# All eight channel groups of branch A as seven products, one filler job per head, one gate tile, two weight and three kq buffers

## The chip, the cores and the metric

The kernel runs on one core of a Trainium2 chip. The metric is the device time of one execution in microseconds (us), from profiler counters on the chip; for the kernel before it is the median of three runs. Engines: PE is TensorE (matmuls; PEld its weight loads), DVE VectorE, ACT ScalarE, POOL GpSimd, SP SyncE, which issues most DMAs.

## The reference, cut to what matters

One layer, for a prompt of 1024 rows and for 8 sample rows (1032 in all), in fp32. Only this much bears on the change:

```
h    = rmsnorm(x, norm_pre) * (1 + scale) + shift
proj = h @ w_in                      # 1024 -> 10256 columns
hA, cA, bA, zA, qkv, zB, beta, alpha, gA, gB = split(proj)
a_conv = causal conv of width 3 over (cA * hA)
yA = ((bA * a_conv) * silu(zA)) @ w_out_a
q, k, v = split(silu(causal conv of width 4 over qkv))      # 8 heads of 128
o, S = gated delta rule over each head (a chain over the rows)
yB = (rmsnorm(o) * silu(zB)) @ w_out_b
merged = sigmoid(gA) * yA + sigmoid(gB) * yB
y  = x + gate * rmsnorm(merged @ w_o, norm_post)
```

hA, cA, bA and zA have 1024 columns each: eight groups of 128 channels. The last rows of the convolutions and the states S are outputs too.

## The kernel before, in words

**Precision.** Each fp32 operand of a large matmul is split into a high and a low part (fp32r), so a product is three matmuls: high by high, low by high, high by low. x is held as xh and xl, a weight as whi and wlo.

**Jobs.** A job (`run`, line 692) projects x on 128 columns of w_in: three groups of 344 rows, eight k blocks, three terms, 72 matmuls of 128x128 by 344 columns into the PSUM tile `pm_t`, of which there are four. While job i runs, the weights of job i+2 are loaded (`w_load`, 671, tile `wraw`, three buffers) and those of i+1 are split (`w_split`: whi by ACT, wlo by DVE, two buffers each). After each group of 24 matmuls a function of the job evacuates it. The list of jobs is built at lines 1358 to 1372, 60 in all: for each head h six jobs, namely k, q, v, two of the 16 column blocks of the merge gates (`gate_job`, 1132: three copies by ACT to a tile and a store) and z (`zb_job`, 1118: three silus by ACT into the gate tile `sz`, two buffers); then three channel groups of branch A (`branch_a_jobs`, 1146; SG = 3) with four jobs each (h, c, b, z).

**Head chains.** Behind the jobs of a head run generators. `qkv_job` (800) copies a projection to `raw`, and does the convolution and the silu into `kq` (k and q, two buffers) or vT; the k of head h waits until head h-2 is done. `decay_gen` (837) makes the decay factors DA and DB with exponentials on ACT. `delta_gen` (864) transposes k and q, squares them (`junk`, `ssk`), makes the 128x128 matrices of the eight chunks, inverts them by blocks (tiles Tw, Tn, Un, T11, U, Qs; not before head h-1 is done), and then goes through the chunks in a chain. For each chunk:

```
pk, po = kq.T @ S          # PE "pa_t<-S,kq", two matmuls
X  = pk * nx + vp          # DVE
pv = U.T @ X               # PE "pa_t<-X,U"
vn = copy(pv)              # ACT
pS, po += kd, DA by vn     # PE "pa_t<-vn,kd" and "pa_t<-vn,DA"
S  = S * egl + pS          # DVE
on, so = copy(po), sum of squares    # ACT
```

After the eighth chunk the flag "done" is set; then come the norm (`rsqrt`, a row of small DVE steps on so and ro), the scaling of `on` (1024 columns, DVE), eight transposes on PE (`pa_t<-ident,on`) and two passes on DVE that multiply by the head's gate `sz`; then the flag "out". `zb_job` makes head h's gate only when "out" of head h-2 is set, as there are two tiles. `sample_gen` (1208) and `sample_norm_gen` (1275) do the same for the sample rows with z_s, a copy of z's last columns.

**Order.** A planner (`Sched`, `Strand`) keeps a clock per engine by its own cost table. After each k block `slot()` runs a step of every generator that is due by the planner's PE clock; `force(cond)` advances them until a condition holds. The generators' PE steps so fall between the projection matmuls, and the tile framework then orders each engine's instructions. PE, ACT, DVE and SP each work through theirs in order; all instructions carry the line of one helper, L121.

**Products.** The other five channel groups (t = 3 to 7) are not jobs. `products` (1575) computes, for each, the four 128-column blocks by Strassen's scheme in Winograd's form: x (two halves of rows by two of k) times four weight blocks in seven half-size products P1, P2, P6, P7, P4, P5, P3. Each product has 48 matmuls of 258 columns, a group 336. `weight_gen` (1404) loads and combines the weights (also from the `wraw` tag: `wsum`), `block_gen` (1493) builds the sums of x blocks T1 to T4 (tiles thi, tlo), DVE adds the products (`evacuate`), and `finish_group` does the convolution and gating. `to_products` is hooked three jobs before the end of the list and first drains the head generators. Then `products_b` (1633) does yB @ w_out_b the same way (14 units; weights and yB blocks come by DMA), then eight jobs follow for w_out_a, and last w_o with the post norm by blocks of rows.

Of the kernel before, what the change touches and what calls it, by code (L numbers as in the profile page):

```python
# [8 lines left out]
F32 = mybir.dt.float32  # L9
# [7 lines left out]
P = 128  # L17
D = 1024
NK = 8
S = 1024  # L20
NB = 8
NT = S + NB
NH = 8
# [6 lines left out]
CY = S + 4 * NB  # L30
UW = 2 + S + 3 * NB
UY = S + 3 * NB
COL_H, COL_C, COL_B, COL_Z, COL_Q, COL_K, COL_V = 0, 1024, 2048, 3072, 4096, 5120, 6144
# [7 lines left out]
SAME = 130.0  # L41
CROSS = 60.0
SLK = 450.0
SG = 3
NAW = 8
NAH = 3
FG = (4, 1, 1, 1)
# [106 lines left out]
def hybrid_step(  # L154
# [13 lines left out]
    wpool = ctx.enter_context(tc.tile_pool(name="weights", bufs=2, side="left"))  # L168
# [97 lines left out]
    smp = dram.tile([2, NB, NH], F32, name="smp")  # L266
# [404 lines left out]
    def w_load(jobs, i):  # L671
        if i >= len(jobs):
            return
        w_ap, c0, n = jobs[i][0:3]
        raw = wpool.tile([P, NK, P], F32, tag="wraw", name="wraw", bufs=3)
        SY.dma_start(out=raw[:, :, :n], in_=w_ap[0, :, c0:c0 + n].rearrange("(k p) c -> p k c", p=P))
        wq[i] = [raw, None, None]

# [113 lines left out]
    flags = {}  # L792
# [7 lines left out]
    def qkv_job(c0, t, ready, dst, post):  # L800
        ri = nraw[0] % 2
        nraw[0] += 1

        def evac(gi, g0, gn, ps):
            raw = raws[ri]
            if gi == 0:
                force(lambda: not busy[ri])
            win = raw[:, 3 + S:CW].rearrange("p (b w) -> p b w", w=4)
            n = min(gn, S - g0)
            A.copy(out=raw[:, 3 + g0:3 + g0 + n], in_=ps[:, :n])  # L810
            if gi == 2:
                GP.tensor_copy(out=win[:, :, 0:3], in_=hist_q[:, t, :].rearrange("p (b w) -> p b w", w=3))
            if n < gn:
                A.copy(out=win[:, :, 3], in_=ps[:, n:gn])
                A.copy(out=last_q[:, t, :], in_=ps[:, n - 3:gn])

        def after():
            busy[ri] = True
            start(gen())

        def gen():
            while not ready():
                yield
            d, raw = dst(), raws[ri]
            act(d, raw[:, 0:CY], AF.Copy, scale=tap_b(t, 0))
            yield 0.0
            for w in range(1, 4):
                for a, b in CHV:
                    stt(d[:, a:b], raw[:, w + a:w + b], tap_b(t, w), d[:, a:b], ALU.mult, ALU.add)
                yield 0.0  # L830
            busy[ri] = False
            act(d, d, AF.Silu)
            post(d)

        jobs.append((w_in, c0, P, x_src, None, evac, after))
# [263 lines left out]
    def head_jobs(h):  # L1099
        st = {}  # L1100

        def kdst():
            st["kq"] = bp.tile([P, 2, CY], F32, tag="kq", name="kq", bufs=2)
            return st["kq"][:, 0, :]

        qkv_job(COL_K + h * P, 8 + h, lambda: h < 2 or flags.get(("done", h - 2)), kdst,
                lambda d: start(decay_gen(h, st)))
        qkv_job(COL_Q + h * P, h, lambda: "kq" in st, lambda: st["kq"][:, 1, :], lambda d: st.update(q=True))

        def vpost(d):  # L1110
            st["v"] = d
            start(delta_gen(h, st))

        qkv_job(COL_V + h * P, 16 + h, lambda: "q" in st and T4.ready(), lambda: T4.get("vT", CY), vpost)

        return st

    def zb_job(h, st):
        def z_evac(gi, g0, gn, ps):
            if gi == 0:  # L1120
                force(lambda: h < 2 or flags.get(("out", h - 2)))
                st["szt"] = bp.tile([P, NT], F32, tag="sz", name="sz", bufs=2)
            act(st["szt"][:, g0:g0 + gn], ps[:, :gn], AF.Silu)

        def z_after():
            V.tensor_copy(out=z_s[:, h, :], in_=st["szt"][:, S:NT])
            st["sz"] = st["szt"]

        jobs.append((w_in, COL_ZB + h * P, P, x_src, None, z_evac, z_after))
# [143 lines left out]
        flags["smp", h] = True  # L1273

    def sample_norm_gen():
        while not flags.get(("smp", NH - 1)):
            yield
        W = NH * NB
        osf = os_all.rearrange("p h b -> p (h b)")
        t_ = bp.tile([P, W], F32, name="sn_t")  # L1280
        tt(t_, osf, osf, ALU.mult)
        yield
        pt = ps_aux()
        PE.matmul(pt[:, 0:W], lhsT=ones, rhs=t_, start=True, stop=True)
        ts(t_, pt[:, 0:W], 1.0 / C, EPS, ALU.mult, ALU.add)
        ro = rsqrt(bp, t_, P, W, "rso")
        tt(osf, osf, ro, ALU.mult)
        stt(yB_s, os_all, onorm, z_s, ALU.mult, ALU.mult)
        store(yBsc[:, :, S:NT].rearrange("h p n -> p h n"), yB_s)
# [66 lines left out]
        jobs[i] = (w_ap, c0, n, src, (lambda: (before() if before else None, f())), evac, after)  # L1356

    gates = [(COL_GB, t, gBsc) for t in range(NK)] + [(COL_GA, t, gAsc) for t in range(NK)]
    for h in range(NH):
        i0 = len(jobs)  # L1360
        st_h = head_jobs(h)
        if h:
            hook(i0, lambda h=h: start(sample_gen(h - 1)))
        for g in gates[2 * h:2 * h + 2]:
            gate_job(*g)
        zb_job(h, st_h)
    iga = len(jobs)
    pools = {}
    T = {}
    for t in range(SG):  # L1370
# [33 lines left out]
    def weight_gen(raw):  # L1404

        sums = {}
        for n, (key, p, g) in enumerate(UNITS):
            a11, a12, a21, a22 = ((key, o, hf, g) for o in range(2) for hf in range(2))
            src = {"P1": a11, "P2": a12, "P6": a11, "P7": a21, "P4": a22, "P5": None, "P3": a12}[p]
            yield from when(lambda: unit[0] >= n - 1, lambda: src is None or src in raw)  # L1410
            hi_ = wpool.tile([P, NK, P], F32R, tag="whi", name="whi", bufs=2)
            lo_ = wpool.tile([P, NK, P], F32R, tag="wlo", name="wlo", bufs=2)
            hi, lo = (v.rearrange("p k c -> p (k c)") for v in (hi_, lo_))
            v = raw[src] if src else sums.pop(g)
            A.copy(out=hi, in_=v)
            yield
            tt(lo, v, hi.bitcast(F32), ALU.subtract)
            made[key, p, g] = (hi_, lo_)
            yield
            if p == "P2":  # L1420
                yield from when(lambda: a22 in raw and a21 in raw)
                s_ = wpool.tile([P, NK, P], F32, tag="wraw", name="wsum", bufs=3)
                s_ = sums[g] = s_.rearrange("p k c -> p (k c)")
                tt(s_, raw[a21], raw[a22], ALU.add)
                yield
                tt(raw[a21], raw[a11], raw[a21], ALU.subtract)
                tt(raw[a11], s_, raw[a11], ALU.subtract)
                yield
                tt(raw[a12], raw[a12], raw[a11], ALU.subtract)
            elif p in ("P6", "P7", "P4", "P3"):  # L1430
                T4.give(raw.pop(src))
# [299 lines left out]
    for t in range(NK):  # L1731
        st = {}
# [168 lines left out]
```

## Time and profile before

| what | value |
|---|---|
| median of 3 runs | 1424.73 us (1422.47 to 1425.23) |
| the profiled execution | 1422.29 us, its span 1420.6 us |
| PE, PEld busy | 1396.6 and 1341.2 us |
| DVE, ACT, POOL busy | 937.7, 658.0, 36.5 us |
| bytes moved by DMA | 161.76 MB |
| granted TensorE clock, mean | 0.997 |

The span is that of the profiled execution between its first and last record. A row of a group reads: line, engine, operation, tile written <- tiles read, partitions x elements out <- in, count | busy us, mean ns of one | idle us ahead of it and what ended it. A row of the timeline reads: start, duration, engine, line, operation, tiles, shape, number of instructions taken together, and in brackets a wait ahead of it with its releaser.

### The profile page before, as it was taken

What the parts mean: (1) busy time and instruction counts of PE and PEld (TensorE: products, weight loads), DVE (VectorE), ACT (ScalarE), POOL (GpSimd) and SP (SyncE); (2) the same over time, 40 slices, a digit from 0 to 9 for tenths busy, and PEclk for the clock granted to TensorE, in tenths of its full rate; (3) what the DMA queues carried; (4) which work ended last, traced back from release to release, by engine and by line L of the source; (5) the groups of instructions that cost most, each with busy time, mean ns of one, the idle gap of its engine ahead of it and who ended that gap; (6) DMA issues with size and microseconds to landing.
All of it is one profiled execution on the core that took longest, in us unless ns stands there. A gap on an engine that the chain in (4) does not pass through costs nothing.

```text
span 1420.6 us, 25886 instructions
## 1 busy us (share of the span) xinstructions
PE 1396.6 (98%) x10130; PEld 1341.2 (94%) x10130; DVE 937.7 (66%) x2444; ACT 658.0 (46%) x1521; POOL 36.5 (3%) x72
## 2 busy tenths in 40 slices
PE   6999999999999999999999999999999999999997
PEld 4899999999999999999999999999999999999786
DVE  6754846758468494494764816978977857864553
ACT  6767453845529465284573332343333344532211
POOL 0000000000001000010000000000000200000000
PEclk9999999999999999999999999999999999999999
DMA  9523352233323333324232323255621875643221
GB/s 321 147 48 94 91 118 71 80 86 93 87 70 106 87 84 94 72 76 106 62 110 69 85 62 86 95 176 170 207 76 31 248 250 182 231 151 93 95 85 59
DMA packets 191396, 161.76 MB, mean 114 GB/s; under 512 B 34311, under 2 KB 166816, under 8 KB 191266
## 3 DMA queue, kind: packets, MB, share of 16 engines
q1 hardware_dynamic: 186720, 151.58, 36.3%
q0 software_dynamic: 4352, 8.46, 2.0%
q8 instruction: 79, 1.29, 0.4%
q14 instruction: 43, 0.35, 0.1%
q10 hardware_dynamic: 202, 0.08, 0.0%
HBM read 123.40 MB, written 36.91 MB: 113 GB/s over the span
## 4 chain that ended last, share of the span: by engine, by line
PE 91%; DVE 5%; DMA 3%; ACT 1%; SPq 0%; issue 0%; DVEq 0%; ACTq 0%
PE pm_t L121 66%; PE pa_t L121 22%; PE pb L121 2%; DVE kq L121 1%; DMA xs<-in_x_prompt_dram 1%; DMA yraw<-yAsc 1%; DMA wor<-in_w_o_dram 0%; DVE S L121 0%; SPq L121 0%; DMA sg<-gAsc 0%; DVE wlo L121 0%; DVE Tw L121 0%; DVE Ttmp L121 0%; DMA sg<-gBsc 0%; DVE ml L121 0%
## 5 line engine op out<-in xcount | busy, mean ns | idle before, releaser
L121 PE MATMUL pm_t<-xh,whi 128*128 128x344 f32 (+1 forms) x1576 | 520.1, 330 | 0.0
L121 PE MATMUL pm_t<-xl,whi 128*128 128x344 f32 (+1 forms) x1576 | 498.1, 316 | 0.0
L121 PE MATMUL pm_t<-xh,wlo 128*128 128x344 f32 (+1 forms) x1576 | 498.1, 316 | 0.0
L121 PEld LDWEIGHTS pm_t<-xh,whi 128*128 128x128 f32 x1576 | 297.0, 188 | 2.0
L121 PEld LDWEIGHTS pm_t<-xl,whi 128*128 128x128 f32 x1576 | 297.0, 188 | 0.2
L121 PEld LDWEIGHTS pm_t<-xh,wlo 128*128 128x128 f32 x1576 | 296.3, 188 | 0.1
L121 DVE TENSOR_TENSOR wlo<-wraw,whi 128x512 fp32r<-128x512 f32 x136 | 92.0, 687 | 49.6 <-ACT whi L121 49.3
L121 ACT CAST whi<-wraw 128x512 fp32r<-128x512 f32 x136 | 82.7, 624 | 75.9 <-PE pm_t L121 73.3
L121 ACT CAST whi<-wr 128x1024 fp32r<-128x1024 f32 x42 | 44.0, 1047 | 84.6 <-PE pm_t L121 40.7
L121 DVE SCALAR_TENSOR_TENSOR kq<-raw,vecs,kq 128x528 f32<-128x528 f32 x96 | 69.2, 761 | 1.9 <-ACT kq L121 1.9
L121 PE MATMUL pm_t<-thi,wlo 128*128 128x258 f32 x240 | 67.9, 283 | 0.1
L121 PE MATMUL pm_t<-thi,whi 128*128 128x258 f32 x240 | 67.7, 282 | 0.0
L121 PE MATMUL pm_t<-tlo,whi 128*128 128x258 f32 x240 | 67.7, 282 | 0.0
L121 PE MATMUL pa_t<-thi,whi 128*128 128x258 f32 x224 | 64.0, 286 | 1.2 <-ACT whi L121 1.2
L121 PE MATMUL pa_t<-thi,wlo 128*128 128x258 f32 x224 | 64.1, 286 | 0.8 <-DVE wlo L121 0.8
L121 PE MATMUL pa_t<-tlo,whi 128*128 128x258 f32 x224 | 63.7, 285 | 0.0
L121 PE MATMUL pm_t<-yhi,whi 128*128 128x344 f32 x192 | 61.5, 321 | 0.0
L121 PE MATMUL pm_t<-ylo,whi 128*128 128x344 f32 x192 | 61.4, 321 | 0.0
L121 PE MATMUL pm_t<-yhi,wlo 128*128 128x344 f32 x192 | 61.3, 320 | 0.0
L121 DVE TENSOR_TENSOR wlo<-wr,whi 128x1024 fp32r<-128x1024 f32 x42 | 51.2, 1219 | 14.5 <-ACT whi L121 14.5
L121 DVE TENSOR_TENSOR Ttmp<-Tw,At 128x60 f32<-128x60 f32 (+24 forms) x248 | 51.9, 209 | 8.8 <-DMA At<-sA 3.7
L121 ACT ACTIVATE junk<-pa_t 128x128 f32<-128x128 f32 x192 | 53.8, 280 | 5.6 <-PE pa_t L121 2.7
(407 smaller groups left out, 2837.2 us busy)
## 6 DMA issues: line engine op xcount, KB each, us to landing
wraw<-in_w_in_dram SPq DMA_DIRECT2D x60, 512.0 KB
wr<-in_w_in_dram SPq DMA_DIRECT2D x40, 256.0 KB
aw<-in_ada_w_dram SPq DMA_DIRECT2D x16, 512.0 KB
gBsc<-gate SPq DMA_DIRECT2D x8, 516.0 KB
gAsc<-gate SPq DMA_DIRECT2D x8, 516.0 KB
txs<-phi SPq DMA_DIRECT2D x8, 516.0 KB
txs<-plo SPq DMA_DIRECT2D x8, 516.0 KB
tlo<-txs POOLq DMA_DIRECT2D x8, 516.0 KB, 8.1
```

The lines of the kernel that those rows point to most:

```text
L121: r = f(*args, **kw)
```

## The change

- SG goes from 3 to 0: all eight channel groups of branch A go through `products`; the twelve jobs of the first three are gone, so there are 48 jobs.
- A new table FILL gives each head one gate job where it had two. The other eight gate jobs come behind the last head.
- The z job of head h-1 stands at the end of head h's jobs, and that of the last head behind the second gate job after the heads. Heads 1 to 7 have so five jobs (k, q, v, gate, z of the head before), head 0 four, and nine jobs follow the last head.
- `sz` has one tile: the z job of head h waits for "out" of head h-1.
- `kq` has three buffers, and the k of head h waits for "done" of head h-3.
- `wraw` has two buffers.
- `sample_norm_gen` also waits for the z of the last head.

```diff
-SG = 3
+SG = 0
+FILL = (1, 1, 1, 1, 1, 1, 1, 1)
...
-        raw = wpool.tile([P, NK, P], F32, tag="wraw", name="wraw", bufs=3)
+        raw = wpool.tile([P, NK, P], F32, tag="wraw", name="wraw", bufs=2)
...
-            st["kq"] = bp.tile([P, 2, CY], F32, tag="kq", name="kq", bufs=2)
+            st["kq"] = bp.tile([P, 2, CY], F32, tag="kq", name="kq", bufs=3)
...
-        qkv_job(COL_K + h * P, 8 + h, lambda: h < 2 or flags.get(("done", h - 2)), kdst,
+        qkv_job(COL_K + h * P, 8 + h, lambda: h < 3 or flags.get(("done", h - 3)), kdst,
...
-                force(lambda: h < 2 or flags.get(("out", h - 2)))
-                st["szt"] = bp.tile([P, NT], F32, tag="sz", name="sz", bufs=2)
+                force(lambda: h < 1 or flags.get(("out", h - 1)))
+                st["szt"] = bp.tile([P, NT], F32, tag="sz", name="sz", bufs=1)
...
+            flags["z", h] = True
...
-        while not flags.get(("smp", NH - 1)):
+        while not flags.get(("smp", NH - 1)) or not flags.get(("z", NH - 1)):
...
+    stz = []
     for h in range(NH):
         i0 = len(jobs)
-        st_h = head_jobs(h)
+        stz.append(head_jobs(h))
...
-        for g in gates[2 * h:2 * h + 2]:
-            gate_job(*g)
-        zb_job(h, st_h)
+        for _ in range(FILL[h]):
+            gate_job(*gates.pop(0))
+        if h:
+            zb_job(h - 1, stz[h - 1])
     iga = len(jobs)
+    for n, g in enumerate(gates):
+        gate_job(*g)
+        if n == 1:
+            zb_job(NH - 1, stz[NH - 1])
...
-                s_ = wpool.tile([P, NK, P], F32, tag="wraw", name="wsum", bufs=3)
+                s_ = wpool.tile([P, NK, P], F32, tag="wraw", name="wsum", bufs=2)
```

PE's order, before, within the chunk chain of head 3 (xh, xl, whi, wlo are the projection's operands; X,U and vn,kd steps of the chain):

```order
L121 MATMUL pa_t<-X,U 128x128
L121 MATMUL pm_t<-xh,whi 128x344
L121 MATMUL pm_t<-xl,whi 128x344
L121 MATMUL pm_t<-xh,wlo 128x344
L121 MATMUL pm_t<-xh,whi 128x344
L121 MATMUL pm_t<-xl,whi 128x344
L121 MATMUL pm_t<-xh,wlo 128x344
L121 MATMUL pa_t<-vn,kd 128x128
L121 MATMUL pa_t<-vn,DA 128x128
```

Six projection matmuls stand here between X,U and vn,kd. PE's order, after, within the chunk chain of head 2 (the helper's line is now 122):

```order
L122 MATMUL pa_t<-vn,kd 128x128
L122 MATMUL pa_t<-vn,DA 128x128
L122 MATMUL pm_t<-xh,wlo 128x344
L122 MATMUL pm_t<-xh,whi 128x344
L122 MATMUL pa_t<-S,kq 128x128 x2
L122 MATMUL pm_t<-xl,whi 128x344
L122 MATMUL pm_t<-xh,wlo 128x344
L122 MATMUL pa_t<-X,U 128x128
L122 MATMUL pm_t<-xh,whi 128x344
L122 MATMUL pm_t<-xl,whi 128x344
L122 MATMUL pm_t<-xh,wlo 128x344
L122 MATMUL pa_t<-vn,kd 128x128
```

Two or three projection matmuls stand between one step of the chain and the next. ACT's order, before, around a z job (sz written from pm_t, three times; vn, on and junk belong to a chunk chain that runs beside it):

```order
L121 ACTIVATE sz_4580<-pm_t_4491 128x344
L121 COPY vn_4586<-pa_t_4584 128x128
L121 COPY on_4582<-pa_t_4604 128x128
L121 ACTIVATE junk_4609,so_4583<-pa_t_4604 128x128
L121 ACTIVATE sz_4580<-pm_t_4598 128x344
```

The first third of z is made in the middle of a chunk chain, ahead of a vn copy. ACT's order, after, around the z job of head 3 (T11 and U belong to head 3's inverse, DA and DB are head 4's exponentials, junk and ssk the squares of head 4's k):

```order
L122 ACTIVATE sz_5014<-pm_t_4729 128x344
L122 COPY T11_724<-pa_t_5065 32x8x32
L122 ACT_TABLE_LOAD
L122 ACTIVATE DB_4959<-DB_4959 128x1024
L122 ACTIVATE DA_4960<-DA_4960 128x1024
L122 ACTIVATE junk_5090,ssk_5083<-pa_t_5085 128x128
L122 ACT_TABLE_LOAD
L122 ACTIVATE sz_5014<-pm_t_5016 128x344
L122 ACTIVATE junk_5092,ssk_5083<-pa_t_5085 128x128
L122 COPY U_723<-pa_t_5103 32x8x32
L122 ACTIVATE junk_5094,ssk_5083<-pa_t_5085 128x128
L122 ACTIVATE sz_5014<-pm_t_5127 128x344
```

The first third of z now waits for the gating of the head before; two table loads, two exponentials and copies of the inverse stand between the first and the last third.

## The prediction

> **What bounds the kernel now.** I read the page first: the busy times and the chain that ended last.
>
> ```profile
> span 1420.6 us, 25886 instructions
> PE 1396.6 (98%) x10130; PEld 1341.2 (94%) x10130; DVE 937.7 (66%) x2444; ACT 658.0 (46%) x1521; POOL 36.5 (3%) x72
> PE 91%; DVE 5%; DMA 3%; ACT 1%; SPq 0%; issue 0%; DVEq 0%; ACTq 0%
> ```
>
> PE is busy 98% of the span and carries 91% of the chain. So the kernel takes as long as PE's matmuls do, plus what PE waits. The table by stretches comes next: heads with the first branch-A jobs, the last four branch-A jobs, five groups as seven products, and the yB products.
>
> ```profile
> 69.30:885.00 815.70, 815.06 (x6107) 796.93 (x6106) 510.85 (x1677) 425.42 (x1180) 18.59 (x28) 1.00 0.31 83
> 885.00:930.00 45.00, 45.00 (x288) 45.00 (x287) 42.67 (x63) 16.93 (x28) 0.00 (x0) 1.00 0.36 116
> 930.20:1131.30 201.10, 201.10 (x1682) 201.04 (x1681) 163.56 (x257) 69.88 (x96) 3.69 (x5) 1.00 0.49 150
> 1131.40:1216.20 84.80, 82.74 (x674) 82.11 (x673) 61.32 (x97) 40.74 (x52) 7.89 (x11) 0.98 0.66 215
> ```
>
> After the stretch and its length stand the busy times of PE, PEld, DVE, ACT and POOL, then the granted clock, the DMA share and GB/s. PE is full at clock 1.00 in the first three stretches. DVE is at 63% with the heads and at 81% in the five product groups (163.56 of 201.10), without PE waiting. Only the yB stretch has idle PE, 2.1 us.
>
> **The change part by part.** *Twelve jobs against three product groups.* The timeline of PE gives the edges: the start of the first of the last four jobs, of the first product, and of the yB products.
>
> ```profile
> 884.95 0.32 PE L121 MATMUL pm_t<-xh,whi 128*128 128x344 f32 x1
> ...
> 930.20 0.28 PE L121 MATMUL pm_t<-xh,whi 128*128 128x258 f32 x1
> ...
> 1131.38 0.28 PE L121 MATMUL pm_t<-thi,whi 128*128 128x258 f32 x1
> ```
>
> Four jobs of 72 matmuls take 930.20 - 884.95 = 45.25 us, 11.31 a job, 157.1 ns a matmul. Five groups of 336 take 1131.38 - 930.20 = 201.2 us, 40.24 a group, 119.8 ns a matmul. The change drops 12 jobs (864 matmuls) and adds 3 groups (1008): 120.7 - 135.7 = -15.0 us, all on PE's path. The other PE work of the stage is the same set of instructions. The Trainium skill ("TensorE: Matmul & The Clock Gate", section "Back-to-back issue gap") speaks against this trade: it gives a sustained stream some 81 ns a matmul at 128 columns and 131 ns at 512. Interpolated, an estimate from that page, a group would take 336 x 98 ns = 32.9 us against 288 x 109 ns = 31.4 us, and the change would cost 4.5 us here. The trace has 119.8 against 157.1 ns at these widths, so it does not agree, and the rows decide.
>
> *Where the jobs go.* A head now has five jobs (the first has four) and nine follow the last head, where there were six and twelve. A head's delta chain (inverse, eight chunks, norm, transposes) must therefore fit under fewer projection matmuls. The order on PE shows what gives way: the matmuls between two steps of the chunk chain. Counting the steps S,kq, X,U and vn,kd with three or fewer projection matmuls ahead of them and nothing else, the order has 9 before and 78 now. What such a step costs is seen in the few tight places of before, head 6:
>
> ```profile
> 784.85 0.32 PE L121 MATMUL pm_t<-xl,whi 128*128 128x344 f32 x1
> 785.07 0.49 PE L121 MATMUL pa_t<-S,kq 128*128 128x128 f32 x2
> ...
> 786.78 0.32 PE L121 MATMUL pm_t<-xh,wlo 128*128 128x344 f32 x1
> 786.98 0.49 PE L121 MATMUL pa_t<-vn,kd 128*128 128x128 f32 x2
> ...
> 788.54 0.40 PE L121 MATMUL pm_t<-xh,whi 128*128 128x344 f32 x1
> 788.94 0.46 PE L121 MATMUL pa_t<-X,U 128*128 128x128 f32 x2
> ```
>
> A matmul is followed 0.157 us later when nothing waits. S,kq behind two of them came after 0.22 us: 0.06 late. vn,kd behind three came after 0.20: 0.04 late. X,U behind one came after 0.40: 0.24 late. Of the 78 steps now 58 are like the first two, two are like the third, and 18 are X,U behind two matmuls, for which I take 0.10, between the rows. 58 x 0.04 + 18 x 0.10 + 2 x 0.24 = 4.6 us, less the 9 that were there (0.5): +4.1 us. The ends are 0 (69 more steps hidden) and 0.24 each, +16.6 us.
>
> *One gate tile.* The z job of head h-1 stands at the end of head h and its first activation waits until head h-2's output has been gated, because there is one tile sz. Behind it on ACT are queued (the order shows it for the job of head 3) the copies and exponentials of the next head, the other two thirds of z and the copy of the next k. PE waits for them through its four pm banks: three hold z, the fourth the next k. The gate's release comes by this chain: last vn, copy and squares on ACT, eleven small DVE steps, the scaling, eight transposes, two gating passes. The rows of before for its parts, grouped, and the wait that it showed once:
>
> ```profile
> L121 ACT ACTIVATE junk<-pa_t 128x128 f32<-128x128 f32 x192 | 53.8, 280 | 5.6 <-PE pa_t L121 2.7
> L121 ACT ACTIVATION_READ_ACCUMULATOR junk<-pa_t 128x1 f32 x192 | 38.4, 200 | 0.0
> L121 ACT COPY on<-pa_t 128x128 f32<-128x128 f32 x64 | 17.0, 266 | 59.0 <-PE pa_t L121 58.9
> L121 DVE SCALAR_TENSOR_TENSOR ro_a<-ro_a,so 128x8 f32<-128x8 f32 x24 | 4.0, 165 | 0.1
> L121 DVE TENSOR_TENSOR on<-on,ro_y 128x1024 f32<-128x1024 f32 x8 | 9.7, 1218 | 0.0
> ```
> ```profile
> 619.35 0.32 PE L121 MATMUL pm_t<-xh,wlo 128*128 128x344 f32 x1
> 620.17 1.09 PE L121 MATMUL pa_t<-ident,on 128*128 128x128 f32 x8 [0.49 <-DVE on L121]
> ...
> 793.73 0.39 PE L121 MATMUL pa_t<-vn,DA 128*128 128x128 f32 x2
> ...
> 800.09 1.08 PE L121 MATMUL pa_t<-ident,on 128*128 128x128 f32 x8
> ```
>
> The parts sum to 0.27 + 0.28 + 0.20 + 11 x 0.165 + 1.22 = 3.8 us at least. The shortest seen from the last vn,DA to the transposes is 800.09 - 793.73 = 6.4 us. In the order of the change three heads (0, 2 and 4) have 20 to 22 projection matmuls in between, with 8 or 16 small products, some 3.1 to 3.5 us plus less than 1. So PE waits between nothing and 2.5 us there, three times. The one wait of the kind in before was 0.82 - 0.16 = 0.66 us. After the transposes the bank is still held for the two gating passes and the activation, and at head 3's z job the order has a table load, two exponentials and another table load between the first and the second third of z:
>
> ```profile
> L121 DVE SCALAR_TENSOR_TENSOR on<-pa_t,vecs,sz 128x512 f32<-128x512 f32 x16 | 11.7, 745 | 2.8 <-PE pa_t L121 2.8
> L121 ACT ACT_TABLE_LOAD x33 | 42.3, 1283 | 17.3 <-DMA sg<-gBsc 5.9 <-DVE kq L121 3.7 <-DVE ban L121 2.5
> L121 ACT ACTIVATE DB<-DB 128x1024 f32<-128x1024 f32 x8 | 8.5, 1061 | 0.1
> L121 ACT ACTIVATE sz<-pm_t 128x344 f32<-128x344 f32 x24 | 10.9, 456 | 18.9 <-PE pm_t L121 18.6
> ```
>
> That is 1.28 + 1.06 + 1.06 + 1.28 + 0.46 = 5.1 us against the 3.8 us that one bank's 24 matmuls last: 1.3 us once. I put 0.9 us on each of the three places, nearest to the row at 620.17: +2.7 us; ends 0 and 3 x 2.5 + 1.3 = 8.8. Two table loads more on ACT (the order has 35) are nothing beside ACT's 46%.
>
> *Two weight buffers, three kq.* A load now waits for the split of two jobs earlier, not three. The tightest case of before is the end of a split and the cast two jobs later; the last row is the median landing of a transfer of the same size in the crowded yB stretch.
>
> ```profile
> 625.09 0.68 DVE L121 TENSOR_TENSOR wlo<-wraw,whi 128x512 fp32r<-128x512 f32 x1
> ...
> 637.82 0.60 ACT L121 CAST whi<-wraw 128x512 fp32r<-128x512 f32 x1
> ```
> ```profile
> thi<-txs POOLq DMA_DIRECT2D x8, 516.0 KB, 9.0
> ```
>
> 637.82 - 625.77 = 12.0 us, 3 more than 9.0, so the load stays hidden: 0. Uncovered it would be up to 2 us at a few jobs. The load waits at the head of SP's queue as it does before, with the chain's small transfers behind it. Three kq buffers let the k convolution of a head start without waiting for the third head back; this only adds slack.
>
> *Into the products.* The last head's output now has 41 us of matmuls (3.7 jobs) until the products begin, where it had 930.20 - 878.56 = 51.6. The blocks T2 to T4 of the first group are built in that time:
>
> ```profile
> 878.56 0.75 DVE L121 SCALAR_TENSOR_TENSOR on<-pa_t,vecs,sz 128x512 f32<-128x512 f32 x1 [1.73 <-PE pa_t L121]
> ...
> 925.18 2.71 DVE L121 TENSOR_TENSOR tlo<-qb,thi 128x516 fp32r<-128x516 f32 x4 [0.69 <-ACT thi L121]
> ```
>
> The last block was done at 927.9 and is used in the fifth product, 23 us after 930.20: 25 us to spare, of which some 11 are lost. Cost 0. *The yB products* lose the early load of w_out_a (512 KB), moved behind; the two PE waits there are 2.0 us.
>
> ```profile
> 1161.93 0.39 PE L121 MATMUL pa_t<-thi,whi 128*128 128x258 f32 x1 [1.23 <-ACT whi L121]
> 1163.19 0.58 PE L121 MATMUL pa_t<-thi,wlo 128*128 128x258 f32 x1 [0.75 <-DVE wlo L121]
> ```
>
> Less traffic could take them away, another order of the transfers could double them: 0, ends -2 and +2.
>
> Sum: -15.0 + 4.1 + 2.7 = -8.2 us. The profiled execution took 1422.29 us (span 1420.6), 2.44 below the median of 1424.73; it would come to 1414.1, and the median to **1416.5 us**.
>
> **The rivals.** *Everything hidden:* steps and gate fit, and only -15.0 is left, 1409.7 us. For it: in before waits at chain steps are some hundredths with two or three matmuls between. Against: 78 such steps.
>
> *The gate stops PE for each head:* seven z jobs wait, each 2.2 us (the 6.4 us row less some 4.2 us of cover): +15.4, 1425.1 us, no change. For it: the tile is single and ACT has other work behind it. Against: in the order the transposes of heads 1, 3 and 5 have 45 to 78 matmuls ahead of them.
>
> *The chain pays at every step (slower):* heads 0, 2, 6 and 7 run chunks with seven matmuls in all, about 7 x 0.157 + five small fp32 products = 2.2 us a chunk; if DVE or ACT is in the middle of something else each time, a step loses the 0.24 us of 788.94: 69 x 0.24 + 2.7 - 15.0 = +4.3, 1429.0 us. It decides from (15.0 - 2.7) / 69 = 0.18 us a step. For it: head 6's chunks have the next head's inverse on DVE between them. Against: the other rows above, 0.04 and 0.06.
>
> *The new products are not cheaper:* if a matmul costs the same at 258 columns as at 344, 144 more of them cost 144 x 0.157 = +22.6 us, 1447. This is the direction of the page cited above. The five groups already measured speak against it almost completely.
>
> **How the numbers follow.** The forecast has 0.62, everything hidden 0.22, the gate 0.07, the paying chain 0.08, dear products 0.01. A measurement of this kernel tells about 0.2%, 2.85 us, from no change. The forecast's own ends (-13 to -4) lie wholly on the faster side, as does everything hidden; of the gate's case some 0.02 does: faster 0.86. Same is the rest of the gate's, 0.05, slower 0.09. The range goes from 1408 (everything hidden and the yB waits shorter) to 1421.5 (forecast with the steps at 0.10 each, 6.9, and the gate near its upper end); the slower cases beyond it and a little below are the 2 in 10.
>
> **What would show it.** Right: PE's eight groups at 40.2 us each, 322 us in one stretch; the heads' stretch shorter by 12 x 11.31 less 4 to 9 us; small idle PE ahead of transposes of on for heads 0, 2 and 4, released by DVE, and ahead of the first matmul of a bank, released by ACT sz. Wrong: product groups over 41 us, idle PE at X,U or vn,kd of 0.2 us and more each, PE waiting for whi or wraw after a load, or a first group that waits for thi.

## The result and the profile after

| | before | after |
|---|---|---|
| median | 1424.98 us (4 runs, 1422.47 to 1426.13) | 1445.06 us (4 runs, 1440.71 to 1448.63) |
| ratio | | 1.0142, 95% interval 1.0110 to 1.0174 |
| profiled execution | 1422.29 us | 1448.63 us |
| heads: second job to first product | 860.9 us | 766.0 us |
| first product to the end | 490.4 us | 611.7 us |

The change made the kernel 20 us slower, where 8 us faster was forecast. The profiled execution after is the slowest of its four and that of before the fastest, so the two profiles lie 26 us apart and what is read from them explains those 26 us. One of the four runs of e3_five below took 1540.14 us at a granted clock of 0.846 and is left out of its median. The page of the kernel after, its span, busy times and chain:

```profile
span 1446.8 us, 26352 instructions
PE 1403.9 (97%) x10274; PEld 1334.7 (92%) x10274; DVE 994.6 (69%) x2516; ACT 673.7 (47%) x1532; POOL 28.7 (2%) x72
PE 46%; DVE 8%; DMA 4%; issue 1%; ACT 1%; SPq 0%; DVEq 0%; ACTq 0%
```

PE still counts as busy for 97%. The shares of the chain sum to 60% and not to 100% as before, since it could be followed back only to 567.19 us, so the 46% of PE is not to be set beside the 91% of before. The table by stretches (heads; eight groups as products; the yB products), with PE, PEld, DVE, ACT and POOL busy, the granted clock, DMA share and GB/s:

```profile
69.10:835.10 766.00, 747.45 (x5530) 715.75 (x5529) 520.96 (x1664) 421.27 (x1163) 10.76 (x28) 0.98 0.32 85
835.10:1159.50 324.40, 323.16 (x2690) 322.35 (x2689) 251.98 (x403) 106.61 (x151) 5.13 (x7) 1.00 0.39 120
1159.50:1241.80 82.30, 81.15 (x674) 80.95 (x673) 61.63 (x97) 40.78 (x52) 6.48 (x9) 1.00 0.65 203
```

The eight groups take 324.4 / 8 = 40.55 us each (40.24 forecast), and the yB stretch 82.3 us (84.8 before). Everything behind the heads is as forecast: 611.7 against 490.4 + 3 x 40.24 = 611.1. The loss is in the heads alone. Before, their 860.9 us were 59 jobs of 11.31 us and 193.5 us of small products, which is what the jobs leave of the stretch. After, 47 jobs and the same small products would be 725.1 us; the stretch has 766.0. **The excess is 40.9 us**, where 4.1 + 2.7 = 6.8 were forecast. Three parts of it can be read. First the waits that a row names, in the table of PE's waits over the heads (sum, times, longest; before, the same table has one row of 0.5):

```profile
PE pa_t L122 <- DVE S L122: 5.0, 4, 3.0
PE pa_t L122 <- ACT U L122: 4.2, 1, 4.2
PE pm_t L122 <- ACT sz L122: 3.7, 3, 1.8
PE pa_t L122 <- DVE kql L122: 1.6, 1, 1.6
PE pa_t L122 <- DVE on L122: 1.2, 3, 0.6
PE pa_t L122 <- DVE kd L122: 1.1, 1, 1.1
PE pa_t L122 <- DVE X L122: 1.0, 2, 0.6
PE pm_t L122 <- ACT gate L122: 0.5, 1, 0.5
```

They sum to 18.3 us, 4.9 of them (sz, on) at the gate. Second, the clock, which was 1.00 in all the heads before. The table by stretches, cut at the four periods in which it is not:

```profile
241.24:248.06 6.82, 5.88 (x24) 5.88 (x25) 0.64 (x2) 1.96 (x7) 0.40 (x1) 0.50 0.24 38
275.37:278.78 3.41, 3.41 (x23) 3.29 (x22) 1.09 (x1) 3.37 (x6) 0.00 (x0) 0.50 0.00 0
490.41:493.82 3.41, 3.00 (x12) 2.56 (x11) 3.11 (x13) 2.17 (x6) 0.00 (x0) 0.50 0.00 0
753.24:766.89 13.65, 13.65 (x84) 12.61 (x79) 0.57 (x3) 4.61 (x13) 0.00 (x0) 0.50 0.09 38
```

27.3 us at half clock, at most 13.7 us lost. Third, a rest of 40.9 - 18.3 - 13.7 = 8.9 us.

Two of the named waits show how they come about. The first is the 4.2 us on U, on the timelines of ACT and PE after the change:

```profile
234.11 0.58 ACT L122 COPY Qs<-pa_t 64x512 f32<-64x512 f32 x1 [1.75 <-PE pa_t L122]
240.60 1.04 ACT L122 CAST kqh<-kq 128x1024 fp32r<-128x1024 f32 x1 [5.91 <-DVE Ttmp L122]
241.56 0.57 ACT L122 COPY U<-pa_t 64x512 f32<-64x512 f32 x1
...
242.18 0.80 PE L122 MATMUL pa_t<-vp,U 128*128 128x128 f32 x2 [4.19 <-ACT U L122]
```

ACT's next instruction after Qs of head 0 was a cast kqh, the fifth of sixteen and so head 2's. It stood 5.91 us for DVE's loop Ttmp, head 1's, which reads At, the tile that a transfer fills for the inverse; kqh, the high part of k and q, and At are tiles of the same pool of six. The copy of U of head 0, which PE needed, stood behind it. The second is the 3.0 us on S, on the timelines of DVE and PE after the change:

```profile
480.35 0.35 DVE L122 SCALAR_TENSOR_TENSOR X<-pa_t,nx,vp 128x128 f32<-128x128 f32 x1
485.07 0.19 DVE L122 TENSOR_TENSOR Ttmp<-Tw,At 128x31 f32<-128x31 f32 x1 [4.38 <-DMA At<-sA]
489.01 0.34 DVE L122 SCALAR_TENSOR_TENSOR S<-S,egl,pa_t 128x128 f32<-128x128 f32 x1
...
489.41 0.71 PE L122 MATMUL pa_t<-S,kq 128*128 128x128 f32 x4 [3.02 <-DVE S L122]
```

DVE stood 4.38 us at the first step of the next head's loop, whose transfer At was not there, and went on with that loop; the S step of the chunk chain came behind it. These two are 7.2 us; the waits on S that are left, on kql, kd, X and gate, 6.2 us together, are not followed up here.

### The profile page after: what moved, and what is told of

It is laid out like the page before. It is cut to its first block, busy times and chain, and to the rows that moved or that the text cites. A ratio compares the mean times of both kernels' runs of the same rounds, so it can differ in the third digit from the quotient of the medians.

```text
span 1446.8 us, 26352 instructions
## 1 busy us (share of the span) xinstructions
PE 1403.9 (97%) x10274; PEld 1334.7 (92%) x10274; DVE 994.6 (69%) x2516; ACT 673.7 (47%) x1532; POOL 28.7 (2%) x72
## 4 chain that ended last, share of the span: by engine, by line
PE 46%; DVE 8%; DMA 4%; issue 1%; ACT 1%; SPq 0%; DVEq 0%; ACTq 0%
PE pm_t L122 33%; PE pa_t L122 14%; DVE acc L122 2%; DVE wlo L122 2%; DVE mrg L122 1%; DMA wr<-in_w_in_dram 1%; DMA yAsc<-acc 1%; DMA Tn<-sT 1%; DMA sg<-gBsc 1%; DVE wr L122 1%; DMA At<-sA 0%; SPq L122 0%; DMA pb__10477<-yBsc 0%; DVE plo L122 0%; DMA txs<-phi 0%
## 5 line engine op out<-in xcount | busy, mean ns | idle before, releaser
L122 PE MATMUL pm_t<-xh,whi 128*128 128x344 f32 (+1 forms) x1384 | 452.2, 327 | 4.2 <-ACT sz L122 3.7
L122 PE MATMUL pm_t<-xl,whi 128*128 128x344 f32 (+1 forms) x1384 | 439.3, 317 | 0.0
L122 PE MATMUL pm_t<-xh,wlo 128*128 128x344 f32 (+1 forms) x1384 | 439.0, 317 | 0.0
L122 PEld LDWEIGHTS pm_t<-xh,whi 128*128 128x128 f32 x1384 | 262.9, 190 | 6.8 <-ACT sz L122 4.4
L122 PEld LDWEIGHTS pm_t<-xl,whi 128*128 128x128 f32 x1384 | 263.1, 190 | 0.5
L122 PEld LDWEIGHTS pm_t<-xh,wlo 128*128 128x128 f32 x1384 | 262.8, 190 | 0.3
L122 PE MATMUL pa_t<-tlo,whi 128*128 128x258 f32 x304 | 85.9, 283 | 0.0
L122 PE MATMUL pa_t<-xh,wlo 128*128 128x258 f32 x256 | 72.5, 283 | 0.3 <-DVE wlo L122 0.3
L122 PE MATMUL pa_t<-xh,whi 128*128 128x258 f32 x256 | 72.4, 283 | 0.0
L122 PE MATMUL pa_t<-xl,whi 128*128 128x258 f32 x256 | 72.2, 282 | 0.0
```

What stands on the lines that cost most here:

```text
L122: r = f(*args, **kw)
```

## The experiments

The **packing theory**: five jobs a head instead of six leave too few projection matmuls between the steps of the heads' strands; an instruction of one strand that waits stands ahead of the other's, and small products crowd on PE. The rival is the **gate-tile theory**: the one tile sz and z a head later hold ACT. For all kernels, excess is the heads' stretch less 11.31 us a job and 193.5 us, clock half of the time at half clock, in us of the profiled execution. These four columns are of one execution each, while the runs of one kernel lie up to 16 us apart (e6_kq2), so small differences in them are not to be trusted. In the diffs below lines are shortened to what changed.

| kernel | jobs a head, SG | median us | ratio to before (95%) | excess | named waits | clock | rest |
|---|---|---|---|---|---|---|---|
| before | 6, 3 | 1424.98 | | 0.1 | 0.5 | 0 | -0.4 |
| after | 5, 0 | 1445.06 | 1.0142 (1.0110 to 1.0174) | 40.9 | 18.3 | 13.7 | 8.9 |
| e1_sg3 | 5, 3 | 1462.12 | 1.0269 (1.0228 to 1.0309) | 41.8 | 12.5 | 20.5 | 8.8 |
| e2_six | 6, 3 | 1429.39 | 1.0047 (1.0032 to 1.0062) | 6.8 | 1.3 | 5.1 | 0.3 |
| e3_five | 5, 3 | 1462.35 | 1.0290 (1.0237 to 1.0343) | 40.3 | 16.6 | 11.9 | 11.8 |
| e4_sz2 | 5, 0 | 1457.00 | 1.0229 (1.0187 to 1.0271) | 44.0 | 19.5 | 11.9 | 12.5 |
| e5_late3 | 5, 0 | 1504.70 | 1.0563 (1.0538 to 1.0588) | 49.6 | 15.6 | 27.3 | 6.7 |
| e6_kq2 | 5, 0 | 1469.16 | 1.0319 (1.0273 to 1.0365) | 60.3 | 24.4 | 27.3 | 8.6 |
| e7_nt7 | 5, 0 | 1437.55 | 1.0112 (1.0077 to 1.0148) | 36.6 | 12.5 | 13.7 | 10.5 |
| e8_six2 | 6, 2 | 1424.17 | 0.9995 (0.9978 to 1.0012) | 4.1 | 0.9 | 3.4 | -0.2 |
| e9_nt7sz2 | 5, 0 | 1444.81 | 1.0143 (1.0123 to 1.0163) | 39.9 | 12.1 | 18.8 | 9.0 |
| e10_mix1 | 6 and 5, 1 | 1430.69 | 1.0042 (1.0027 to 1.0057) | 14.3 | 2.2 | 10.2 | 1.9 |
| e11_mix1nt7 | 6 and 5, 1 | 1446.71 | 1.0153 (1.0132 to 1.0174) | 28.2 | 5.8 | 18.8 | 3.6 |
| e12_bsg2 | 6, 2 | 1425.36 | 1.0009 (0.9999 to 1.0020) | 4.3 | 1.7 | 0 | 2.6 |
| e13_smp1 | 5, 0 | 1425.80 | 1.0019 (1.0004 to 1.0034) | 18.5 | 6.1 | 3.4 | 9.0 |
| e14_smp2 | 5, 0 | 1448.99 | 1.0181 (1.0160 to 1.0202) | 41.2 | 9.3 | 30.7 | 1.2 |
| e15_six2s1 | 6, 2 | 1425.82 | 1.0021 (1.0008 to 1.0033) | 6.6 | 2.6 | 0 | 4.0 |
| e16_bsg2s1 | 6, 2 | 1424.79 | 1.0011 (1.0001 to 1.0021) | 2.7 | 1.1 | 0 | 1.6 |
| e17_f2 | 5, 0 | 1421.57 | 0.9991 (0.9975 to 1.0007) | 20.9 | 3.8 | 8.5 | 8.5 |
| e18_sg1f222 | 6 and 5, 1 | 1428.79 | 1.0027 (1.0016 to 1.0039) | 17.2 | 3.1 | 11.9 | 2.2 |

(A job is one of k, q, v, gates, z; the table counts those of heads 1 to 7. Head 0 has one fewer in the kernels with a late z: in e17 it has five where it had four. So in e18 only heads 1 and 2 have six.)

### The packing or the gate tile: four runs

**e1_sg3**, on the kernel after:

```diff
-SG = 0
+SG = 3
```

> The changed kernel with SG back at 3: five jobs a head, late z and one gate tile stay, only the three channel groups are jobs again. The trace after the change has 40.5 us per product group, against 4 x 11.31 us of jobs, so both theories of the heads (packing, gate tile) expect 15 us more than after the change: 1460 us, between 1455 and 1465. A theory that the loss sits in the way into the longer product stretch expects less than 1445.

1462.12 us, 17.1 more than after the change: the three groups as products are worth what the sum said (15.0), and the excess in the heads is the same with them (41.8) and without (40.9).

**e2_six**, on the kernel after, with a line that places the last z when no gates are left:

```diff
-SG = 0
-FILL = (1, 1, 1, 1, 1, 1, 1, 1)
+SG = 3
+FILL = (2, 2, 2, 2, 2, 2, 2, 2)
```

> The changed kernel with SG = 3 and two gate jobs a head as before (FILL all 2, the last z first behind the heads); one gate tile, late z, three kq and two weight buffers stay. Packing theory (five jobs instead of six leave too few projection matmuls, so that instructions of one head's strand that wait stand ahead of the other's chain steps in the in-order queues): the waits go, 1425 to 1430 us, near the kernel before. Gate-tile theory (z waits for the head before and ACT stands): the waits stay, 1445 to 1460 us.

1429.39 us. Over its heads PE has only these waits, and the one period at half clock:

```profile
PE pm_t L122 <- ACT hA L122: 0.5, 1, 0.5
PE pa_t L122 <- DVE X L122: 0.4, 1, 0.4
PE pa_t L122 <- DVE S L122: 0.2, 1, 0.2
PE pa_t L122 <- ACT vn L122: 0.2, 1, 0.2
```
```profile
211.12:221.36 10.24, 10.24 (x59) 8.99 (x58) 3.27 (x17) 2.50 (x7) 0.00 (x0) 0.50 0.01 2
```

One gate tile, late z, two weight buffers and three kq buffers are all in this kernel, and no wait on sz is left. What it has more than the kernel before (0.47%, 6.7 us) is about the half clock, 10.24 / 2 = 5.1, and the 1.3 us of waits.

**e3_five**, on the kernel before (two gate tiles, z at its own head):

```diff
-        for g in gates[2 * h:2 * h + 2]:
-            gate_job(*g)
+        gate_job(*gates[h])
         zb_job(h, st_h)
     iga = len(jobs)
+    for g in gates[NH:]:
+        gate_job(*g)
```

> The kernel before with one gate job per head and the other eight behind the heads; z at its own head, two gate tiles, two kq, three weight buffers, SG = 3. Packing theory: the heads' stretch loses as it does after the change, 1450 to 1465 us. Gate-tile theory: no loss, 1424 to 1430 us.

1462.35 us: the same loss of 40 us in the heads without any of the other edits. PE's longest rows there:

```profile
PE pm_t L121 <- ACT gate L121: 6.0, 4, 3.4
PE pa_t L121 <- ACT vn L121: 3.4, 2, 3.1
PE pa_t L121 <- DVE Un L121: 2.3, 4, 0.7
```

Other instructions are waited for than after the change, to the same sum. The gate-tile theory falls on both counts: in the heads, five jobs a head cost some 40 us with it or without it, six cost 0 to 7.

**e4_sz2**, on the kernel after (beside three kq buffers a second gate tile has no room):

```diff
-force(lambda: h < 1 or flags.get(("out", h - 1)))
-name="sz", bufs=1
-name="kq", bufs=3      # and h < 3, done h - 3
+force(lambda: h < 2 or flags.get(("out", h - 2)))
+name="sz", bufs=2
+name="kq", bufs=2      # and h < 2, done h - 2
```

> The changed kernel with two gate tiles (z of head h waits for the output of head h-2) and, for the room, two kq buffers; z stays a head later, five jobs a head, SG = 0. Packing theory: only the waits on sz go (3.7 us, and one period of half clock behind one of them, 1.7 us): 1438 to 1446 us. Gate-tile theory: most of the 33 us of excess goes, 1412 to 1425 us.

1457.00 us, slower than either theory had it. It changes two buffers; e6 takes them apart.

### Queues and buffers: four runs

**e5_late3**, on the kernel after, in the planner's clock for a transfer:

```diff
-        self.arrival = self.clk["DMA"] + 700.0
+        self.arrival = self.clk["DMA"] + 3700.0
```

> The changed kernel with one number of the planner raised: it believes that every transfer lands 3 us later (700 to 3700 ns), so instructions that need one are put later in the queues; nothing else changes. If the waits come from DVE and ACT standing at an instruction that needs a transfer still under way, with a chain step behind it (the wait on S behind the 4.4 us for At at 480 us is one), some 5 to 10 us go: 1435 to 1440 us. If they come from the packing alone, however it is ordered: 1441 to 1449 us, as after the change.

1504.70 us, a miss. The heads did not gain (49.6 us of excess), and the products lost most: the stretch from the first of them to the end took 663.6 us against 611.7, and PE waited 42.7 us for whi and wlo there, where it was 2.4. That the waits can be ordered away by such a number is not shown, and the run moved too much to refute that the two quoted waits came from a queue's order.

**e6_kq2** and **e7_nt7**, on the kernel after:

```diff
-name="kq", bufs=3      # and h < 3, done h - 3
+name="kq", bufs=2      # and h < 2, done h - 2
...
-NT4 = 6
+NT4 = 7                # e7_nt7 only
```

> The changed kernel with two kq buffers (k of head h waits for head h-2), the one gate tile left: the reference for the next run, and one half of the run with two gate tiles that gave 1457. If the missing kq buffer cost those 12 us: 1455 to 1459. If the second gate tile did: 1441 to 1449.

> Two kq buffers as in the run before, and seven work tiles of the common pool instead of six (NT4 = 7). If the cast kqh on ACT stands because no tile of that pool is free until the inverse has read At (5.9 us on ACT, 4.2 on PE at 238 us), 5 to 10 us less than with two kq buffers alone. If tiles are not short: within 3 us of it.

1469.16 and 1437.55 us. So with five jobs a head the third kq buffer is worth 24 us (1469.2 - 1445.1), twice the 12 us of the one expectation and against the other; the second gate tile is worth 12 (e4 against e6); and a seventh work tile 32, far more than expected (named waits 24.4 to 12.5, clock 27.3 to 13.7). The reason given for e7 was not tested: in e6, with six work tiles, the cast kqh no longer waits for Ttmp, and its longest wait is 1.8 us, for PE. Why the seventh tile brings so much stays open.

**e9_nt7sz2**, e7_nt7 with the second gate tile of e4_sz2:

> The changed kernel (five jobs a head, SG = 0) with seven work tiles, two gate tiles and two kq buffers. So far, each against two kq buffers alone (1469): a seventh work tile -32, a second gate tile -12. If the packing hurts only through tiles that come back too late, the two together reach the kernel before or better: 1415 to 1426. If what is left is the bare shortage of projection matmuls (short steps of the chain, small products in a row that halve the clock): 1432 to 1438, as with the seventh work tile alone.

1444.81 us, outside both expectations: the gains do not add. Against e7 the named waits are the same (12.1), and the clock takes 5 us more. A theory of short buffers alone falls with it: some 37 to 40 us of excess are left with seven work tiles. That each buffer changes the order of the whole stretch is a likely reason, and not shown.

### Fewer products or fewer jobs: four runs

**e8_six2**, e2_six with SG = 2; **e10_mix1**, on the kernel after; **e11_mix1nt7**, e10 with two kq buffers, two gate tiles, seven work tiles; **e12_bsg2**, the kernel before with SG = 2 alone:

```diff
-SG = 0
-FILL = (1, 1, 1, 1, 1, 1, 1, 1)
+SG = 1                              # e10, e11
+FILL = (2, 2, 2, 2, 2, 2, 1, 1)     # the last z behind the first gate left
```

> Six jobs a head (two gate jobs each, the last z first behind the heads) as in the run that gave 1429.4, with SG = 2: six groups as products, eight branch-A jobs and one z behind the heads. The packing theory has no loss in the heads, and a group fewer of jobs saves 17 / 3 = 5.7 us by the runs with SG 0 and 3: 1422 to 1426 us. If the last head's chain then lacks cover ahead of the products: 1430 or more.

> SG = 1 and two gate jobs for heads 0 to 5, one for heads 6 and 7 (the last z behind the first of the two gate jobs left); one gate tile, three kq, six work tiles. By the runs with SG 3 and 2 and six jobs a head (1429.4, 1424.2) a group less of jobs is worth 5.2: 1419 if the last head's chain, which ended 49 us ahead of the products with SG = 2, still fits; every further 10 us that it stands in the open make it as much slower, up to 1435.

> The run before with two kq buffers, two gate tiles and seven work tiles. If tiles are what the heads run short of, some us less than it: 1413 to 1419. If six jobs a head have no shortage left, the same within 3 us, or more by the missing kq buffer.

> The kernel before with SG = 2 and nothing else: one group more as products, four jobs less behind the last head. The trade alone gives 1424.5 - 5.5 = 1419. The last head's chain ended 51.6 us ahead of the products; with 45 us less the drain of the head chains three jobs ahead of the products comes too early by some 28 us, and the chain then runs with less cover: 1419 to 1435.

1424.17, 1430.69, 1446.71 and 1425.36 us. With six jobs a head a group more as products brings 5.2 us (e8 against e2), as expected, and about what e2 had lost. In e10 the first product group runs short of weights; PE's row there:

```profile
863.33 0.39 PE L122 MATMUL pa_t<-xh,wlo 128*128 128x258 f32 x1 [2.60 <-DVE wlo L122]
```

e11 has a gate tile and a work tile more than e10 and a kq buffer less, and is 16 us slower, 8.6 of it in the clock, 3.6 in named waits. e12 gives its 5 us of trade back: 4.3 in the heads, where the last chain now ends nearer to the products, and 4.1 behind them (534.8 us from the first product to the end, where 490.4 + 40.24 was to be had).

### The clock as a cause of its own: four runs

The timeline of PE after the change, ahead of the longest period at half clock:

```profile
749.84 0.69 PE L122 MATMUL pa_t<-Un,DB 32*32 32x32 f32 x16
750.46 1.09 PE L122 MATMUL pa_t<-ident,on 128*128 128x128 f32 x8
751.49 0.69 PE L122 MATMUL pa_t<-Un,DB 32*32 32x32 f32 x16
752.26 0.59 PE L122 MATMUL pa_t<-Qs,Tn 32*32 32x32 f32 x13
...
753.98 0.66 PE L122 MATMUL pm_t<-xh,whi 128*128 128x344 f32 x1
754.43 0.49 PE L122 MATMUL pm_t<-xl,whi 128*128 128x344 f32 x1
754.72 0.49 PE L122 MATMUL pm_t<-xh,wlo 128*128 128x344 f32 x1
```

PE waited for nothing named. For 4 us it had only small products, then the projection matmuls followed each other in 0.29 us and took 0.49, where they follow in 0.157 and take 0.32. The sample strand's small products can be moved without a change to anything else; **e13_smp1** and **e14_smp2**, on the kernel after:

```diff
-            hook(i0, lambda h=h: start(sample_gen(h - 1)))
+            hook(i0 + 1, lambda h=h: start(sample_gen(h - 1)))    # e14: i0 + 2
```

> The changed kernel with the sample strand of each head started one job later (with the q job in place of the k job); no work is added or left out. By the order on PE no stretch of 3.4 us then holds fewer than three projection matmuls (two stretches with none after the change). If small products in a row set the half clock: the 27.3 us at half clock fall below 14, 1432 to 1440 us. If it only follows the waits, which the move does not aim at: 1441 to 1449.

> The same with the strand two jobs later (with the v job): by the order three stretches of 3.4 us hold at most two projection matmuls. If small products in a row set the half clock: 27 us or more at half clock, 1443 to 1455, slower than with one job by 5 us or more. If not: equal to it.

1425.80 and 1448.99 us. The same projections, the same small products: one job later takes 19 us off, more than expected, two jobs later adds 4. The stretches at half clock in the heads of e13 and, of five in e14, the first, the second and the last:

```profile
198.08:201.49 3.41, 3.41 (x14) 3.41 (x13) 3.41 (x13) 0.08 (x1) 0.00 (x0) 0.50 0.43 95
675.94:679.36 3.42, 3.42 (x17) 3.22 (x16) 1.23 (x9) 0.64 (x3) 0.00 (x0) 0.50 0.25 74
```
```profile
230.46:244.11 13.65, 12.46 (x70) 11.38 (x68) 2.45 (x10) 6.43 (x18) 0.40 (x1) 0.50 0.40 97
264.59:278.25 13.66, 10.76 (x89) 9.64 (x90) 7.55 (x14) 12.91 (x25) 0.00 (x0) 0.50 0.10 40
...
694.67:715.15 20.48, 20.48 (x132) 17.90 (x132) 6.19 (x23) 6.57 (x15) 0.00 (x0) 0.50 0.11 28
```

6.8 us at half clock in e13, 61.4 in e14 (27.3 after the change). And the waits of e14 were half of those after the change:

```profile
PE pa_t L122 <- DVE on L122: 4.9, 5, 3.5
PE pa_t L122 <- DVE kd L122: 1.9, 2, 1.4
PE pa_t L122 <- ACT U L122: 1.2, 1, 1.2
PE pa_t L122 <- DVE sm_rT L122: 1.1, 1, 1.1
PE pa_t L122 <- ACT vn L122: 0.2, 1, 0.2
```

So the half clock does not just follow the waits: e14 has half the waits and more than twice the half clock, and the same time. In e13 the waits went down as well (18.3 to 6.1), so its gain is not the clock's alone: of the 22.4 us that the excess fell, 10.3 are the clock's and 12.2 the waits'.

**e15_six2s1** and **e16_bsg2s1**, the same move by one job in e8_six2 and e12_bsg2:

> Six jobs a head, SG = 2 (1424.2), with the sample strand a job later. Its trace had 6.8 us at half clock at 213 us, where sample products stood among those of the inverse. If they set it: 1419 to 1422. If not: 1424.

> The kernel before with SG = 2 (1425.4), with the sample strand a job later. Its trace had no half clock in the heads, so nothing is to be had from the clock: 1424 to 1427; what it loses lies in the first product group.

1425.82 and 1424.79 us. e15 lost its half clock in the heads (3.4 to 0) as expected, and got 1.7 us of named waits and 4 of rest in exchange; the forecast of 1419 to 1422 missed. e16 is what was expected.

### Towards a version that beats both: two runs

**e17_f2** and **e18_sg1f222**, on e13_smp1:

```diff
-FILL = (1, 1, 1, 1, 1, 1, 1, 1)
+FILL = (2, 1, 1, 1, 1, 1, 1, 1)     # e17
+FILL = (2, 2, 2, 1, 1, 1, 1, 1)     # e18, with SG = 1
```

> The changed kernel with the sample strand a job later (1425.8) and two gate jobs in head 0 (one less behind the heads); SG = 0. In the run before PE waited 3.1 us for DVE at 194 us, where DVE stood 8.2 us for the transfer Tn of head 0's inverse, and lost 1.7 us more to the half clock behind it. If a job more ahead of that point covers the transfer and the last head (whose transposes ended 38 us ahead of the products) still fits: 1419 to 1423. If the wait only moves, or the last head now stands in the open: 1425 to 1432.

> The same with two gate jobs in heads 0, 1 and 2 and SG = 1 (four jobs of branch A more, 5 us of the trade given back). Three of eight heads with six jobs: of the 18.5 us of excess in the heads some 7 go, 1425.8 + 5 - 7 = 1424, between 1420 and 1428.

1421.57 and 1428.79 us. In e17 the wait at 194 us fell from 3.1 to 0.6 us (named waits 6.1 to 3.8), and its profiled execution, at 1428.36 one of its slower ones, had 13.65 us at half clock behind small products at 603 us. Its runs lie between 1417.77 and 1428.85; the ratio, 0.9991 (0.9975 to 1.0007), does not tell it from the kernel before. e18 missed its 1424 us (1420 to 1428): the waits and the rest fell (3.1 and 2.2), but the clock took 11.9 where e13 had 3.4. Of all versions none is faster than the kernel before by more than the measurement tells.

## Why the prediction was wrong, point by point

**Twelve jobs against three groups: right.** 40.55 us a group against 40.24, and e1 has 17.1 us for the trade, 15.0 forecast. The rival of dear products is out.

**The short steps: right in size.** The counted steps of the chunk chain lost what the rows of before said. The timeline of PE after the change, a chunk of head 0:

```profile
251.23 0.32 PE L122 MATMUL pm_t<-xh,wlo 128*128 128x344 f32 x1
251.45 0.71 PE L122 MATMUL pa_t<-S,kq 128*128 128x128 f32 x4
...
252.16 0.32 PE L122 MATMUL pm_t<-xl,whi 128*128 128x344 f32 x1
252.38 0.49 PE L122 MATMUL pa_t<-X,U 128*128 128x128 f32 x2
...
253.03 0.32 PE L122 MATMUL pm_t<-xl,whi 128*128 128x344 f32 x1
253.23 0.49 PE L122 MATMUL pa_t<-vn,kd 128*128 128x128 f32 x2
```

0.22, 0.22 and 0.20 us instead of 0.157: 0.06, 0.06 and 0.04 late, where 0.04 (S,kq behind two, though its row had 0.06), 0.10 (X,U behind two) and 0.04 (vn,kd behind three) were taken. Added up over the heads from the same rows, all steps with three or fewer projection matmuls ahead, at full clock and without a named wait, come 3.7 us late after the change and 0.7 before: +3.0 where 4.1 was forecast. So of the rest of 8.9 us some 6 are not explained here.

**One gate tile: right in kind.** 1.2 us on the transposes of on, at heads 0, 2 and 4 as forecast, and 3.7 on sz, 4.9 against 2.7, within the ends 0 and 8.8. Its longest wait, 1.8, was forecast as 1.3. But e2 has the same tile and no wait on sz: it is a cost of five jobs a head.

**The step that failed: "A head's delta chain must therefore fit under fewer projection matmuls", costed by the latency of single steps.** The sum counted how long a step of one head's chain takes from PE to DVE or ACT and back. It left out that DVE and ACT serve two or three heads' strands in order, and that an instruction of another strand that waits for a transfer or a tile then stands ahead of the step. 18.3 - 4.9 = 13.4 us of named waits had no term; the rows above show this cause for 7.2 of them. DVE waited for At before as well (3.7 us in two places, 7.6 in three after), without PE waiting for it; with six jobs a head e2 has 1.3 us of named waits in all. Fewer jobs alone do not set the size: with the same five jobs and the sample strand moved, e13 has 18.5 us of excess and not 40.9. That the third kq buffer was put at nothing ("this only adds slack") belongs to it: with five jobs a head it was worth 24 us. With six no run takes it alone. What of the weights was put at 0 stayed so: PE has no wait on whi or wlo in the heads. Two weight buffers by themselves were not tried.

**The other missing term: the clock.** "PE is full at clock 1.00" was read as a property of the stage. It hung on the order of the work on PE: with only the sample strand moved, the 27.3 us at half clock became 6.8 (e13) and 61.4 (e14). In the heads, every period at half clock lasted 3.41 us or a multiple of it (6.82, 10.24, 13.65, 17.07, 20.48), and they began behind stretches with few projection matmuls, whether PE waited there (242 us) or ran small products (750 us). The Trainium skill ("TensorE: Matmul & The Clock Gate", Part 1, "What's actually happening") has it that a monitor throttles to half rate after an idle window of about 3.4 us and releases after a busy one. The trace agrees on the half and on the 3.41 us, and shows more: the clock also fell behind 3.41 us that PE filled almost wholly with small products (busy 3.3 us ahead of 753.24). By the rows it cost up to 13.7 us.

**Into the products: right.** No thi wait in the first group; yB lost its two waits of 2.0 us and the 3.41 us at half clock (1163 us) and got one of 1.15 us on wlo at 1236.19, 82.3 against 84.8 us.

**The rivals.** "The chain pays at every step" had the sign and the place, the heads' chunk chains, and 1429 us; its mechanism did not show, since most steps lost 0.04 to 0.06 us and not 0.24. "The new products are not cheaper" had 1447 us, 2 us from the median, by luck: a group takes 40.55 us, and the loss lies elsewhere. The gate at every head did not come. None of the rivals had the two strands in one queue or the clock, and so the range ended 23.6 us below the median.

What stays open: how much of the named waits a better order of DVE and ACT alone would save (e5 moved too much else), and how few large matmuls in 3.41 us the clock stands. Counted in steps of 3.41 us from a fall, in the heads of these kernels it fell behind windows with 0 to 9 of some 22 projection matmuls, and held behind one with none of them, twelve products of 128x128 and 48 small ones (at 432 us after the change). So the number of projection matmuls does not decide it, not even where all else on PE is small: of two windows that PE filled and that had six projection matmuls, the clock fell behind the one with 53 small products (e2, from 207.71 us) and held behind the one with 70 (e7, from 203.85 us).

## What to carry to other kernels

Matmuls that hide a side chain are not only work: before you trade them for cheaper ones, count what each stage needs as cover, with the in-order queues of every engine that serves two chains, and try the thinner cover alone (e3 was one small edit and showed the whole loss). Where small products fill PE, look at the granted clock by stretches as well as at waits; moving a group of them by one job was worth 19 us here, by fewer waits and less half clock, and by two jobs it cost 4. And with a planner between, one buffer more does not act alone: the same seventh work tile gained 32 us in one version and, with a second gate tile, only 12 in another.

## What the chip showed that was not expected

PE's clock can halve without any wait, behind some 3.4 us that small products fill for the most part (e2: 10.24 us at half clock with 1.3 us of named waits in the whole of the heads). It does not always do so (e7 at 203.85 us). A busy PE in the table is no sign of a full clock: the stretch 753.24 to 766.89 was busy for 13.65 of 13.65 us at 0.50.
